# Moving the sums behind the norm, pinning adds, aligning pools, and a third seven-product unit per layer, in a two-layer encoder trunk

## The chip, the cores and the metric

The kernel runs on one core of a Trainium2 chip, as one program. The metric is device microseconds (us) of one execution. The engines of the core work side by side, each through its own list of instructions in order: TensorE (PE, matmuls; PEld is its weight loads), VectorE (DVE), ScalarE (ACT), GpSimd (POOL) and SyncE (SP, which here issues the loads). They wait for one another by semaphores.

## What is computed

An encoder trunk of two layers on 256 positions of 2048 channels, all in float32. Each layer has a mixer (pooling and attention in the first, a matrix memory, mLSTM, in the second) and a gated MLP, and this document is about the MLP:

```python
def conv_ffn(x, w_up, conv_w, conv_b, w_down):
    u = x @ w_up
    up = jnp.pad(u, ((0, 0), (1, 1), (0, 0)))
    c = conv_w.astype(u.dtype)
    u = c[0] * up[:, :-2] + c[1] * up[:, 1:-1] + c[2] * up[:, 2:] + conv_b.astype(u.dtype)
    gate, val = jnp.split(u, 2, axis=-1)
    return (jax.nn.silu(gate) * val) @ w_down
...
for layer in range(DEPTH):
    h = rms_norm(x, norm_mix[layer])
    ...
    x = x + mixed
    x = x + conv_ffn(rms_norm(x, norm_ffn[layer]), w_up[layer], conv_w[layer], conv_b[layer], w_down[layer])
```

`w_up` is 2048 x 11264 (two halves of 5632 = 44 tiles of 128), `w_down` 5632 x 2048.

## The kernel before

**Split numbers.** A float32 operand is kept as a high and a low part of a narrower format, and a product is three matmuls: high by high, high by low, low by high. Activations are split once per norm (`xx`, lines 282 and 285: high on ACT, low on DVE).

**The stream of weights.** All weights pass once through `Stream`, in the order in which PE uses them, as chunks of 128 x 1024 floats (512 KB). `load` (L89) issues the transfer on SP's queue into a raw tile `w`; `split` makes the high part on ACT (L105) and the low part on DVE (L106), in a tile `hl`. In an FFN layer there are seven raw tiles and five split ones; `ahead` keeps three split chunks ahead of PE's and issues a load five chunks ahead of the split.

**The FFN layer.** The 44 tiles of `w_up` are done in six groups of 4, 8, 8, 8, 8, 8 (`FCH`), each followed by its part of the down-projection, which is interleaved with the next group's up-projection. `_ffn_plan` writes the order out by hand as a list of slots, one weight chunk each: an up step ("n") has four slots of 16 matmuls, and yields one tile of gate and of value; a down step ("d") of a group and one of four column blocks has two or four slots of 12 matmuls. After an up step comes its tail: `gather` (L382, L383), the norm's row (L927), the convolution, the gate and the split of the result (L908 to L917). After a down step two residual adds (L392).

**Units of seven products.** For the last four tiles of two groups (`UNITS`: groups 2 and 4) the up-projection is not done by four up steps but as one 2 x 2 block product with seven block products in place of eight (`quads`). Its operands are sums of blocks of the activations, made once per layer by `sums()` (L935 to L951; tile `v`, split into `sx`), and sums of blocks of weights, made in place on the raw chunks by DVE in `split`: kind "sum" one add (L99), kind "chain" two (L102, which reads the sum of the chunk before, and L103). A unit has 28 chunks: eight pairs of sum and chain, then twelve of which eight are sums, 75% more loads than the sixteen that four up steps need. Each chunk serves two products of three matmuls (tile `p`). The partial results are put together on ACT and DVE (L993 to L1014), then turned by 16 transposes (L1026) and go through the same tails, by `finish`. `_ffn_plan` spreads a unit's chunks evenly among the slots between two places that `UNITS` gives, with a pause of three slots before the last twelve.

**The norm.** In an FFN layer PE starts before the norm's scale is known. `Norm.finish` computes it: a reduction (L298), a reciprocal square root (L224, a power on POOL at L226, L228 to L231) that gives `rcol`, two diagonals `dg` (L310), and one product with ones, `npr`, that gives the row `R` (L315). `n0` (L1085) is minus the first column of `rcol`.

**Who sets the order.** PE's instructions run as the program is written (`manual_schedule`). What is to happen beside the main stream (`norm.finish`, `sums_ready`, `finish`) is a generator in `Weave`: `add` gives it a delay, `tick` moves the time on with the matmuls issued (0.645 for four matmuls of an up step, 0.68 for three of a product) and runs one step of one generator that is due. The order of ACT's, DVE's and SP's instructions is made by the framework's scheduler from the program's data dependences and its own estimate of the time: it may put an instruction ahead of others that were written before it. `tc.keep_in_program_order(ins)` ties one instruction behind the one that was written just before it on the same engine.

Of the kernel before, what the change touches and what calls it, by code (L numbers as in the profile page):

```python
# [9 lines left out]
F32 = mybir.dt.float32  # L10
# [6 lines left out]
P = 128  # L17
# [47 lines left out]
class Stream:  # L65


    def __init__(self, nc, wpool, spool, srcs, load_ahead, split_ahead):
        self.nc, self.wpool, self.spool, self.srcs = nc, wpool, spool, srcs
        self.la, self.sa = load_ahead, split_ahead  # L70
        self.w, self.hl = {}, {}
        self.n_load = self.n_split = self.at = 0
        self.more = None
# [7 lines left out]
    def load(self, pieces=1):  # L81
        i = self.n_load
        src = self.srcs[i]
        kind, src = src if isinstance(src, tuple) else ("plain", src)
        width = src.shape[-1]
        n = width // pieces
        w = self.home(i, True).tile([P, CH * P], F32, tag="w", name=f"w{i}")
        for c in range(0, width, n):
            self.nc.sync.dma_start(w[:, c : c + n], src[:, c : c + n])  # L89
        self.w[i] = w, n, width, kind  # L90
        self.n_load += 1

    def split(self, then=None):
        i = self.n_split
        w, n, width, kind = self.w.pop(i)
        hl = self.home(i, False).tile([P, 2, CH * P], F32R, tag="hl", name=f"hl{i}")
        l, r = w[:, 0:512], w[:, 512:1024]
        if kind == "sum":
            self.nc.vector.tensor_add(r, r, l)  # L99
            self.sum = r  # L100
        if kind == "chain":
            self.nc.vector.tensor_add(l, l, self.sum)  # L102
            self.nc.vector.tensor_add(r, r, l)  # L103
        for c in range(0, width, n):
            (self.nc.vector.tensor_copy if i + c == 0 else self.nc.scalar.copy)(hl[:, 0, c : c + n], w[:, c : c + n])  # L105
            self.nc.vector.tensor_sub(hl[:, 1, c : c + n], w[:, c : c + n], hl[:, 0, c : c + n].bitcast(F32))  # L106
            then and then(c // n)
        self.hl[i] = hl
        self.n_split += 1

    def ahead(self, i, split=None):
        n = len(self.srcs)
# [14 lines left out]
class Weave:  # L127
# [6 lines left out]
    def add(self, gen, delay=0.0):  # L134
        self.q.append([self.t + delay, gen])
# [37 lines left out]
def trunk(ctx: ExitStack, tc: tile.TileContext, gx, xT, xn, call, catt, cml, weights, out):  # L173
    nc = tc.nc
    v, a, g, pe = nc.vector, nc.scalar, nc.gpsimd, nc.tensor
# [7 lines left out]
    wp = pool("wraw", 6)  # L183
    sp = pool("wsplit", 4)
    smp = pool("small", 2)
    sm1 = pool("small1", 1)
# [5 lines left out]
    gcol = cp.tile([P, NG], F32, tag="gcol", name="gcol")  # L192
    a_x = actp.tile([P, KT, S], F32, tag="B1", name="xT")
    x = xp.tile([P, 2, D], F32, tag="x", name="x")
    st = Stream(nc, wp, sp, weights, 5, 2)

    gx0 = actp.tile([P, NG + 2 * S], F32, tag="B0", name="gx0")
    ctx.enter_context(tc.manual_schedule(engines={mybir.EngineType.PE}))
# [11 lines left out]
    wv = Weave()  # L210
# [34 lines left out]
    class Norm:  # L245
# [48 lines left out]
        def finish(self):  # L294
            n = self.n
            yield from wv.wait(lambda: self.blocks == NB)
            s2 = smp.tile([P, 2], F32, tag="nsum", name=f"nsum{n}")
            v.tensor_reduce(s2, self.ss, AX.X, ALU.add)  # L298
            self.rcol = rsqrt(s2, 2, 1.0 / D, f"n{n}")
            yield 2.5  # L300
            if n % 2 == 0:
                rr = dram.tile([2, P], F32, tag="rr", name=f"rr{n}")
                g.dma_start(rr.rearrange("t p -> p t"), self.rcol)
                R = sm1.tile([P, S], F32, tag="R", name=f"R{n}")
                g.dma_start(R.rearrange("p (t q) -> p t q", t=2), rr.unsqueeze(0).to_broadcast([P, 2, P]))
                self.R = R
                return
            dg = sm1.tile([P, 2, P], F32, tag="dg", name=f"dg{n}")
            for t in range(2):
                v.tensor_scalar_mul(dg[:, t, :], ident, self.rcol[:, t : t + 1])  # L310
            yield 1.0
            pr = psp.tile([P, 512], F32, tag="ps", name=f"npr{n}")
            mm(pr[:, 0:S], ones, dg.rearrange("p a b -> p (a b)"), True, True)
            R = sm1.tile([P, S], F32, tag="R", name=f"R{n}")
            v.tensor_copy(R, pr[:, 0:S])  # L315
            self.R = R
# [571 lines left out]
    def ffn_layer(layer, norm, nxt):  # L888
        with ExitStack() as es:
# [4 lines left out]
            xsp = cp1 = lp(f"fs{layer}", 1)  # L894
# [35 lines left out]
            def sums():  # L930

                vv = actp.tile([P, 2, KT // 2, S], F32, tag="B1", name=f"v{layer}")
                for h in range(2):
                    ks = slice(8 * h, 8 * h + 8)
                    v.tensor_add(vv[:, 0], norm.xx[:, ks, 0, :].bitcast(F32), norm.xx[:, ks, 1, :].bitcast(F32))  # L935
                    yield 5.0
                    q = vv[:, 0].rearrange("p (a k) (t c) -> p a k t c", k=2, t=2)
                    a11, a21, a12, a22 = (q[:, :, k, t, :] for k in range(2) for t in range(2))
                    raw = vv[:, 1].rearrange("p k s -> p (k s)").rearrange("p (j a c) -> p j a c", j=4, a=4)
                    s1, s2, s3, s4 = (raw[:, j] for j in range(4))  # L940
                    v.tensor_sub(s1, a21, a22)
                    v.tensor_add(s3, a11, a21)
                    yield 3.0
                    v.scalar_tensor_tensor(s2, s1, -1.0, a11, ALU.mult, ALU.subtract)
                    v.tensor_sub(s4, s3, a12)
                    v.tensor_sub(s4, s4, a22)
                    yield 4.0
                    for j in range(4):
                        hi, lo = (sx[:, j, 4 * h : 4 * h + 4, i, :] for i in range(2))
                        a.copy(hi, raw[:, j])  # L950
                        v.tensor_sub(lo, raw[:, j], hi.bitcast(F32))  # L951
                        yield 2.0
# [15 lines left out]
            def quads(fs, gt, i0, name):  # L968
# [8 lines left out]
                r0, r1 = norm.rcol[:, 0:1], norm.rcol[:, 1:2]  # L977
                for p in range(m):
                    ends = p == 0, p == m - 1
                    hl = st.next()  # L980
                    if p == 0:
                        b1, b5 = bank(1), bank(5)
                    product(b1, block_of(2 * p, 0), hl, 0, *ends)
                    product(b5, sum_of(0, p), hl, 512, *ends)
                    yield
                    hl = st.next()
                    if p == 0:
                        b6, b4 = bank(6), bank(4)
                    product(b6, sum_of(1, p), hl, 0, *ends)
                    product(b4, block_of(2 * p + 1, 1), hl, 512, *ends)  # L990
                    if p == m - 1:
                        c12, c21, c22 = part(12), part(21), part(22)
                        a.activation(c12, b1, AF.Copy, scale=n0)  # L993
                        a.activation(c21, b1, AF.Copy, scale=r1)
                        a.activation(c22, b5, AF.Copy, scale=r1)
                        v.scalar_tensor_tensor(c12, b6, n0, c12, ALU.mult, ALU.add)
                    yield
# [21 lines left out]
            def finish(top, bottom, fs, gt, i0, name):  # L1019

                for n, f in enumerate(fs):
                    tr = psp.tile([P, 2, S], F32, tag="ps", name=f"tr{layer}_{f}")
                    for j in range(2):
                        for t, src in enumerate((top, bottom)):
                            c = (2 * j + n) * P
                            pe.transpose(tr[:, j, t * P : t * P + P], src[:, c : c + P], ident)  # L1026
                    u = tp.tile([P, 2, S], F32, tag="tb", name=f"tb_{layer}_{f}")
                    a.copy(u, tr)
                    tail(u, f, gt, i0 + n)
                    yield 2.5  # L1030

            def down_end(gt, b, kts):

# [44 lines left out]
            wv.add(norm.finish(), 4.0)  # L1078
            sx = xsp.tile([P, 4, KT // 2, 2, P], F32R, tag="sx", name=f"sx{layer}")

            n0 = xsp.tile([P, 1], F32, tag="n0", name=f"n0_{layer}")

            def sums_ready():
                yield from wv.wait(lambda: norm.R is not None)
                v.tensor_scalar_mul(n0, norm.rcol[:, 0:1], -1.0)  # L1085
                yield from sums()

            wv.add(sums_ready(), 8.0)
            st.la, st.sa, st.more = 7, 3, (lp(f"fw{layer}", 1), lp(f"fh{layer}", 1), st.at + len(_ffn_plan()))
            gts, run = {}, {}  # L1090
            for step in _ffn_plan():
                kind, c = step[:2]
                if kind != "d" and c not in gts:
# [78 lines left out]
    return np.concatenate(out)  # L1172


UNITS = {2: (1, 3), 4: (3, 5)}


def _ffn_plan():

    slots, begin = [], []  # L1180
# [9 lines left out]
    begin.append(len(slots))  # L1190
    here = [[] for _ in slots]
    m = KT // 2
    for c, (c0, c1) in UNITS.items():
        lo, hi = begin[c0] + 2, begin[c1] - 7
        one, two = 2 * m, m + m // 2
        step = (hi - lo - 3) / (one + two)
        for k in range(one + two):
            here[int(lo + k * step + (3 if k >= one else 0))].append(("s", c, 0))
# [148 lines left out]
```

## Time and profile before

| | us |
|---|---|
| three runs | 2223.16, 2224.29, 2226.46 (median 2224.29) |
| the profiled execution | 2224.29, its span (first to last instruction) 2222.0 |
| first FFN layer, first up matmul to first matmul of the mLSTM layer | 255.78 to 998.39 |
| second FFN layer, first up matmul | 1476.05 |
| matmuls of units, `p` | 672, from 322.9 to 2014 |
| granted TensorE clock, mean over the span | 0.995 |

The profile is one execution, taken by the hardware's profiler. Busy time is that of instructions at work; a row of a group gives line, engine, operation, what is written from what with shapes, how many, busy us, mean ns of one, and after the bar the idle time of the engine just before them with what ended it. Weights stream from memory at 198 GB/s on average over the span.

### The profile page before, as it was taken

How to read it: one execution, taken by the hardware profiler on the slowest of the kernel's cores; microseconds unless marked ns; L12 is line 12 of the kernel's file. 1: busy time of each engine (PE TensorE's matmuls, PEld its weight loads, DVE VectorE, ACT ScalarE, POOL GpSimd, SP SyncE). 2: the span in 40 equal slices, each digit the busy share in tenths (PEclk: the TensorE clock that was granted, in tenths of full speed). 3: DMA queues.
4: the chain of work that ended last, by engine and by line, in shares of the span. 5: the costliest groups of instructions: out<-in, count | busy, mean ns of one | idle time of the engine just before them, and what ended most of it. 6: DMA issues, size and time to landing. Idle time of an engine off the chain costs nothing.

```text
span 2222.0 us, 30399 instructions
## 1 busy us (share of the span) xinstructions
PE 2193.0 (99%) x11328; PEld 1864.8 (84%) x11328; DVE 1668.8 (75%) x2378; ACT 1228.3 (55%) x1744; POOL 28.1 (1%) x40
## 2 busy tenths in 40 slices
PE   9999899999999999999999999989999999999999
PEld 7888688888888888889888888868888888888887
DVE  7686778788787787666767666677878878778764
ACT  7675555556555565556555455545555655556552
POOL 0020000000000000000000000000000000000000
PEclk9999999999999999999999999999999999999999
DMA  8545546676666766556555555645667666676553
GB/s 317 187 157 181 170 164 215 209 239 215 217 221 222 222 198 191 188 157 206 163 193 184 185 180 167 198 162 165 213 210 238 217 215 220 223 223 199 190 190 123
DMA packets 124951, 440.88 MB, mean 198 GB/s; under 512 B 13851, under 2 KB 16195, under 8 KB 124803
## 3 DMA queue, kind: packets, MB, share of 16 engines
q1 hardware_dynamic: 121568, 434.93, 59.8%
q10 hardware_dynamic: 3074, 3.75, 0.7%
q8 instruction: 89, 1.46, 0.3%
q0 software_dynamic: 160, 0.26, 0.1%
q14 instruction: 60, 0.48, 0.1%
HBM read 436.74 MB, written 2.14 MB: 198 GB/s over the span
## 4 chain that ended last, share of the span: by engine, by line
PE 85%; DVE 6%; DMA 6%; issue 2%; ACT 0%; DVEq 0%; ACTq 0%
PE up L219 27%; PE dn L219 20%; PE op L219 8%; DMA w<-in_q 6%; PE p L219 5%; PE mv L219 4%; PE mq L219 4%; PE mk L219 4%; PE mo L219 4%; DVE hl L106 3%; PE qproj L219 3%; PE kproj L219 1%; PE pool L219 1%; PE vproj L219 1%; PE qk L219 1%
## 5 line engine op out<-in xcount | busy, mean ns | idle before, releaser
L106 DVE TENSOR_TENSOR hl<-w,hl 128x1024 fp32r<-128x1024 f32 (+1 forms) x820 | 992.3, 1217 | 295.8 <-ACT hl L105 291.7
L105 ACT CAST hl<-w 128x1024 fp32r<-128x1024 f32 (+1 forms) x819 | 851.7, 1047 | 570.6 <-PE up L219 185.5
L219 PE MATMUL up<-xx,hl 128*128 128x512 f32 (+1 forms) x4608 | 829.7, 338 | 1.9 <-DVE hl L106 1.9
L219 PEld LDWEIGHTS up<-xx,hl 128*128 128x128 f32 x4608 | 719.5, 189 | 114.6 <-DVE hl L106 4.8
L219 PE MATMUL dn<-hl,g 128*128 128x512 f32 x2064 | 485.0, 391 | 0.6 <-DVE hl L106 0.6
L219 PEld LDWEIGHTS dn<-hl,g 128*128 128x128 f32 x2064 | 385.2, 188 | 83.2 <-DVE hl L106 1.2
L908 ACT ACTIVATE y<-tb_up,cst 128x256 f32<-128x256 f32 x144 | 78.8, 595 | 84.6 <-DVE tb_up L927 83.5
L219 PE MATMUL p<-hl,sx 128*128 128x512 f32 x384 | 104.2, 393 | 0.0
L99 DVE TENSOR_TENSOR w<-w 128x512 f32<-128x512 f32 x64 | 44.3, 692 | 76.4 <-DMA w<-in_q 76.2
L382 ACT COPY tb_up<-up 128x512 f32<-128x512 f32 x72 | 42.2, 586 | 102.6 <-PE up L219 100.3
L219 PE MATMUL mk<-xx,hl 128*128 128x512 f32 (+1 forms) x512 | 92.2, 337 | 0.0
L219 PE MATMUL mq<-xx,hl 128*128 128x512 f32 (+1 forms) x512 | 92.1, 337 | 0.0
L219 PE MATMUL mv<-hl,xx 128*128 128x512 f32 (+2 forms) x480 | 91.7, 350 | 0.0
L219 PE MATMUL op<-hl,cat 128*128 128x512 f32 x384 | 91.6, 393 | 0.0
L219 PE MATMUL mo<-hl,xx 128*128 128x512 f32 x384 | 90.4, 391 | 0.0
L219 PE MATMUL op<-hl,mcat 128*128 128x512 f32 x384 | 89.5, 392 | 0.0
L219 PEld LDWEIGHTS mq<-xx,hl 128*128 128x128 f32 x512 | 79.2, 188 | 11.6
L219 PEld LDWEIGHTS mk<-xx,hl 128*128 128x128 f32 x512 | 79.0, 188 | 11.4
L219 PEld LDWEIGHTS mv<-hl,xx 128*128 128x128 f32 x480 | 78.3, 189 | 11.2
L219 PEld LDWEIGHTS op<-hl,mcat 128*128 128x128 f32 x384 | 71.5, 188 | 14.6
L219 PEld LDWEIGHTS mo<-hl,xx 128*128 128x128 f32 x384 | 71.0, 188 | 14.1
L219 PEld LDWEIGHTS op<-hl,cat 128*128 128x128 f32 x384 | 70.9, 188 | 14.1
(240 smaller groups left out, 1746.9 us busy)
## 6 DMA issues: line engine op xcount, KB each, us to landing
w<-in_up SPq DMA_DIRECT2D x288, 512.0 KB, 4.1
w<-in_dn SPq DMA_DIRECT2D x176, 512.0 KB, 4.3
w<-in_m_in SPq DMA_DIRECT2D x124, 512.0 KB, 4.1
w<-in_q SPq DMA_DIRECT2D x112, 512.0 KB, 4.2
w<-in_a_in SPq DMA_DIRECT2D x46, 512.0 KB, 4.3
w<-in_a_out SPq DMA_DIRECT2D x32, 512.0 KB, 3.4
w<-in_m_out SPq DMA_DIRECT2D x32, 512.0 KB, 3.5
w<-in_m_g SPq DMA_DIRECT2D x5, 432.0 KB, 3.5
```

The lines of the kernel that those rows point to most:

```text
L99: self.nc.vector.tensor_add(r, r, l)
L105: (self.nc.vector.tensor_copy if i + c == 0 else self.nc.scalar.copy)(hl[:, 0, c : c + n], w[:, c : c + n])
L106: self.nc.vector.tensor_sub(hl[:, 1, c : c + n], w[:, c : c + n], hl[:, 0, c : c + n].bitcast(F32))
L219: pe.matmul(out_, lhsT, rhs, start=start, stop=stop, skip_group_check=True)
L382: a.copy(tb, ps[:, :, 1, :])
L908: a.activation(y[:, j, :], u[:, j, :], AF.Identity, scale=cw(tl, 1), bias=cw(tl, 3))
```

## The change

Four edits. `sums_ready` is started with a delay of 14.0 in place of 8.0, and the first add of each half of `sums()` is tied behind the DVE instruction written before it. The adds on weight chunks move out of `split` into a method `sums`, which `split` calls for its own chunk if that is still to do, and, at its end, for the next chunk; each add is tied. `dg` is allocated 16 floats longer and `n0` 64 floats in place of 1. `UNITS` gets a third unit, of group 5, and places with slot offsets for all three; a unit's first chunk now waits (`late`, in the weave's time, not by a semaphore) until the tails of the unit before have been issued.

```diff
+    def sums(self, i):
+        if i in self.w and not self.w[i][4] and self.w[i][3] != "plain":
+            w, kind = self.w[i][0], self.w[i][3]
+            l, r = w[:, 0:512], w[:, 512:1024]
+            pin, add = self.tc.keep_in_program_order, self.nc.vector.tensor_add
+            if kind == "sum":
+                pin(add(r, r, l))
+                self.sum = r
+            if kind == "chain":
+                pin(add(l, l, self.sum))
+                pin(add(r, r, l))
+            self.w[i][4] = True

     def split(self, then=None):
         i = self.n_split
-        w, n, width, kind = self.w.pop(i)
+        self.sums(i)
+        w, n, width = self.w.pop(i)[:3]
...
-        if kind == "sum":
-            self.nc.vector.tensor_add(r, r, l)
-            self.sum = r
-        if kind == "chain":
-            self.nc.vector.tensor_add(l, l, self.sum)
-            self.nc.vector.tensor_add(r, r, l)
...
         self.hl[i] = hl
         self.n_split += 1
+        self.sums(i + 1)
...
-            dg = sm1.tile([P, 2, P], F32, tag="dg", name=f"dg{n}")
+            dg = sm1.tile([P, 2 * P + 16], F32, tag="dg", name=f"dg{n}")[:, : 2 * P]
+            dg = dg.rearrange("p (t q) -> p t q", t=2)
...
-                    v.tensor_add(vv[:, 0], norm.xx[:, ks, 0, :].bitcast(F32), norm.xx[:, ks, 1, :].bitcast(F32))
+                    tc.keep_in_program_order(
+                        v.tensor_add(vv[:, 0], norm.xx[:, ks, 0, :].bitcast(F32), norm.xx[:, ks, 1, :].bitcast(F32)))
...
                 for p in range(m):
                     ends = p == 0, p == m - 1
+                    if p == 0:
+                        wv.until(lambda: not late)
+                        late.update((0, 2))
...
                     tail(u, f, gt, i0 + n)
                     yield 2.5
+                late.discard((i0 - 4) % 4)
...
-            n0 = xsp.tile([P, 1], F32, tag="n0", name=f"n0_{layer}")
+            n0 = xsp.tile([P, 64], F32, tag="n0", name=f"n0_{layer}")[:, 0:1]
...
-            wv.add(sums_ready(), 8.0)
+            wv.add(sums_ready(), 14.0)
...
-            gts, run = {}, {}
+            gts, run, late = {}, {}, set()
...
-UNITS = {2: (1, 3), 4: (3, 5)}
+UNITS = {2: (1, 2, 2, 20), 4: (3, 0, 4, 20), 5: (4, 23, 5, 24)}
...
-    for c, (c0, c1) in UNITS.items():
-        lo, hi = begin[c0] + 2, begin[c1] - 7
+    for c, (c0, d0, c1, d1) in UNITS.items():
+        lo, hi = begin[c0] + d0, begin[c1] + d1
```

`begin[c]` is the slot at which group c starts: 0, 16, 56, 88, 136, 168 in both kernels, and the list ends at 216 before, at 200 after (four up steps of group 5 are gone), with sixteen slots of the last down step behind it.

More of the change, by code (lines that the diff above doesn't have):

```diff
@@ L65, with __init__ @@
 class Stream:
-    def __init__(self, nc, wpool, spool, srcs, load_ahead, split_ahead):
-        self.nc, self.wpool, self.spool, self.srcs = nc, wpool, spool, srcs
+    def __init__(self, tc, wpool, spool, srcs, load_ahead, split_ahead):
+        self.tc, self.nc, self.wpool, self.spool, self.srcs = tc, tc.nc, wpool, spool, srcs
         self.la, self.sa = load_ahead, split_ahead
@@ L89, in load @@
             self.nc.sync.dma_start(w[:, c : c + n], src[:, c : c + n])
-        self.w[i] = w, n, width, kind
+        self.w[i] = [w, n, width, kind, False]
         self.n_load += 1
+    def sums(self, i):
[10 more added lines that the diff above has]
+            self.w[i][4] = True
     def split(self, then=None):
         i = self.n_split
-        w, n, width, kind = self.w.pop(i)
+        self.sums(i)
+        w, n, width = self.w.pop(i)[:3]
         hl = self.home(i, False).tile([P, 2, CH * P], F32R, tag="hl", name=f"hl{i}")
-        l, r = w[:, 0:512], w[:, 512:1024]
-        if kind == "sum":
-            self.nc.vector.tensor_add(r, r, l)
-            self.sum = r
-        if kind == "chain":
-            self.nc.vector.tensor_add(l, l, self.sum)
-            self.nc.vector.tensor_add(r, r, l)
         for c in range(0, width, n):
@@ L194, in trunk @@
     x = xp.tile([P, 2, D], F32, tag="x", name="x")
-    st = Stream(nc, wp, sp, weights, 5, 2)
+    st = Stream(tc, wp, sp, weights, 5, 2)
     gx0 = actp.tile([P, NG + 2 * S], F32, tag="B0", name="gx0")
```

## The prediction

> **What bounds the kernel now.** I read the page's engine summary first, then the waits of TensorE (PE), then the order of instructions around the one long wait, then the chain of waits for the pace of each kind of matmul, and last the stretches in which VectorE (DVE) is fullest.
>
> ```profile
> span 2222.0 us, 30399 instructions
> PE 2193.0 (99%) x11328; PEld 1864.8 (84%) x11328; DVE 1668.8 (75%) x2378; ACT 1228.3 (55%) x1744; POOL 28.1 (1%) x40
> ```
>
> PE is busy all but 29 us, so the time is PE's work plus its few gaps. PE's waits (total us, times, longest):
>
> ```profile
> PE npr L219 <- DVE n L1085: 21.3, 2, 10.7
> PE up L219 <- DVE hl L106: 1.9, 5, 0.8
> ...
> PE dn L219 <- DVE hl L106: 0.6, 2, 0.4
> ```
>
> Almost all of it is one matmul, `npr`, which spreads the FFN norm's row over the partitions, once per FFN layer. The order of time around the first one (start, us, engine, line):
>
> ```profile
> 260.76 5.14 PE L219 MATMUL up<-xx,hl 128*128 128x512 f32 x28
> 276.56 1.19 PE L219 MATMUL npr<-dg,cst 128*128 128x256 f32 x2 [10.66 <-DVE n L1085]
> ```
>
> ```profile
> 257.18 2.28 DVE L935 TENSOR_TENSOR v<-xx 128x2048 f32<-128x2048 f32 x1
> ...
> 260.52 0.15 DVE L298 TENSOR_REDUCE nsum<-nss 128x2 f32<-128x8 f32 x1
> 260.59 0.68 DVE L941 TENSOR_TENSOR v<-v 128x512 f32<-128x512 f32 x1
> 261.19 0.69 DVE L942 TENSOR_TENSOR v<-v 128x512 f32<-128x512 f32 x1
> 261.79 1.22 DVE L106 TENSOR_TENSOR hl<-w,hl 128x1024 fp32r<-128x1024 f32 x1
> 262.93 0.48 DVE L285 SCALAR_TENSOR_TENSOR xx<-xt,gcol,xx 128x256 fp32r<-128x256 f32 x1
> 263.32 0.16 DVE L224 TENSOR_SCALAR rv_n<-nsum 128x2 f32<-128x2 f32 x1
> ...
> 267.72 0.15 DVE L228 TENSOR_TENSOR re_n<-ry_n 128x2 f32<-128x2 f32 x1
> ...
> 275.94 0.48 DVE L310 TENSOR_SCALAR dg<-cst,re_n 128x128 f32<-128x128 f32 x2
> ```
>
> The chain L298, L224, L228 to L231, L310 is seven tiny steps, but between every two of them DVE has been given a long one, mostly from `sums()` (L935 to L951). PE runs dry at about 265.9 and waits 10.66 us for a chain that is some 2 us of work. The clock then lags (columns: window, its us, busy us and counts of PE, PEld, DVE, ACT, POOL, granted clock, DMA share, GB/s):
>
> ```profile
> 275.00:280.00 5.00, 3.44 (x10) 2.90 (x11) 4.82 (x11) 1.64 (x3) 0.00 (x0) 0.50 0.00 0
> 280.00:285.00 5.00, 5.00 (x28) 4.35 (x28) 3.05 (x5) 3.16 (x5) 0.00 (x0) 0.93 0.01 3
> ...
> 1495.00:1500.00 5.00, 3.17 (x9) 2.63 (x10) 5.00 (x13) 1.91 (x4) 0.00 (x0) 0.50 0.00 0
> 1500.00:1505.00 5.00, 5.00 (x24) 4.36 (x23) 2.53 (x5) 2.56 (x4) 0.00 (x0) 0.73 0.00 0
> ```
>
> **The change, part by part.**
>
> *Sums behind the norm's row.* `sums_ready` starts 14 instead of 8 ticks into the layer, and the first add of each half (L935) is pinned behind whatever DVE instruction was traced before it. For the first half that is `n0`, which reads `rcol`, the end of the chain; the rest of `sums()` reads what L935 wrote. So nothing of `sums()` can stand between the chain's steps any more. What is left for DVE from 257.2 to 265.9, 8.7 us, are three or four splits (L106), four L285 and the chain. From row to row above, starts lie 0.60 apart for a 512-wide operation, 1.14 for a split and 0.39 for L285: 4 x 1.14 + 4 x 0.39 + about 1 = 7.1 us, which fits. The wait of 21.3 us goes, and so does the half clock: 3.44 us at 0.50 cost 1.7 and 5.00 us at 0.93 cost 0.35; 3.17 and 5.00 us at 0.50 and 0.73 cost 1.6 and 1.35. That is 5.0 in both layers. What may remain of the wait is 0 if the chain is through in time, 3 us a layer if each step still loses a split; I take 0.5.
>
> The Trainium skill (TensorE: Matmul & The Clock Gate, "HAM oscillation") says that gaps of PE over about 3.4 us let the gate fall back to half, and that it takes some 3.4 us of work to lift it again. By it the clock's part would be 2 x 1.7 = 3.4 us, 1.6 less than these rows give, and a leftover gap below 3.4 us would cost no clock; no row of this trace shows one between 1 and 10 us to try it on. I keep the rows.
>
> The sums themselves don't vanish: a half is 2.2 (L935) and nine operations of 0.6, 7.6 us, so 15.2 a layer, of which DVE did nearly all while PE stood. Now they lie beside the up-projections. The prices, from the groups (busy, mean ns, idle before), each less the 0.08 that starts overlap:
>
> ```profile
> L909 DVE SCALAR_TENSOR_TENSOR y<-tb_up,cst,y 128x255 f32<-128x255 f32 x144 | 63.6, 478 | 0.0
> ...
> L99 DVE TENSOR_TENSOR w<-w 128x512 f32<-128x512 f32 x64 | 44.3, 692 | 76.4 <-DMA w<-in_q 76.2
> ...
> L915 DVE TENSOR_TENSOR y<-y 128x256 f32<-128x256 f32 x88 | 36.9, 420 | 1.1 <-ACT y L914 0.9
> ```
>
> A slot (one weight chunk) of an up step costs DVE a split, 1.14, and a quarter of the tail (two at 0.61, four at 0.40, two at 0.34), 0.87: 2.01 us. A down slot costs 1.14 + 2 x 0.6 / 4 = 1.44. A unit's chunk costs 2.05 in its first sixteen (a split and 1.5 adds of 0.61) and 1.55 in the last twelve. The second half of the sums is needed by the unit's ninth chunk, slot 33. From slot 4 to there DVE has 28 up slots, 2 down slots, 8 unit chunks and the sums: 56.3 + 2.9 + 16.4 + 15.2 = 90.8 us, while PE has 28 x 2.79 + 2 x 2.74 + 8 x 1.38 = 94.6 (paces below). 96% full: between 0 and some 4 us a layer; I take 1.5, since three split chunks (8 us) are kept ready ahead of PE. What queues behind a pinned L935 is splits and tails; PE waits for the splits first.
>
> *The third unit.* PE's paces, from the chain of waits and the order of time:
>
> ```profile
> 885.12 22.29 PE up L219 x128
> 907.41 10.99 PE dn L219 x48
> ```
>
> ```profile
> 329.90 0.86 PE L219 MATMUL p<-hl,sx 128*128 128x512 f32 x3
> 330.60 0.86 PE L219 MATMUL p<-hl,xx 128*128 128x512 f32 x3
> 331.30 5.72 PE L219 MATMUL up<-xx,hl 128*128 128x512 f32 x32
> ...
> 533.16 0.60 PE L1026 MATMUL tr<-cst,c 128*128 128x128 f32 x4
> 533.52 2.36 PE L219 MATMUL up<-xx,hl 128*128 128x512 f32 x12
> ```
>
> An up step is 64 matmuls, 11.15 us (2.79 a slot); a down slot is 10.99 / 4 = 2.74. A unit chunk is six matmuls: 1.40 us from start to start here, 12 x 10.99 / 48 / 2 = 1.37 at the down pace; 1.38. Four up steps (44.6) become 28 chunks (38.6) and 16 transposes (four take 0.36: 1.4). A unit saves 4.6 +- 0.5, two units 9.
>
> It costs 12 more chunks per layer, loaded and split. By the plan's arithmetic the layer's chunks 4 and 5 begin at slots 136 and 168, so the new unit lies on slots 159 to 192, one unit chunk to 1.07 slots, where the old two have one to 2.14 and 2.43 (now 1.96 and 2.32). That stretch has 16 up slots, 17 down slots and 28 unit chunks. PE: 44.6 + 46.6 + 38.6 = 129.8 us. DVE: 32.2 + 24.5 + 32.8 + 18.6, five operations on the partial results (3.1) and the four tails of the unit before (4 x 2.28 = 9.1): 120.3 us, 93%. Can DVE do that without holding PE? Windows of the present units, same columns:
>
> ```profile
> 438.00:548.00 110.00, 109.38 (x554) 92.19 (x554) 91.67 (x125) 67.03 (x89) 0.00 (x0) 1.00 0.70 228
> ...
> 460.00:480.00 20.00, 20.00 (x97) 16.65 (x96) 17.28 (x23) 11.36 (x14) 0.00 (x0) 1.00 0.83 275
> 480.00:500.00 20.00, 20.00 (x103) 16.95 (x102) 14.62 (x17) 10.14 (x12) 0.00 (x0) 1.00 0.69 224
> 500.00:520.00 20.00, 20.00 (x104) 16.99 (x103) 13.87 (x16) 9.93 (x12) 0.00 (x0) 1.00 0.77 254
> 520.00:540.00 20.00, 20.00 (x105) 17.04 (x104) 18.97 (x29) 14.70 (x23) 0.00 (x0) 1.00 0.68 219
> 540.00:560.00 20.00, 20.00 (x101) 16.86 (x101) 20.00 (x36) 13.78 (x23) 0.00 (x0) 1.00 0.52 176
> ```
>
> For 40 us it ran at 97% with PE at 20.00 of 20, but over 110 us nothing has asked more than 83% of it. I take 2 us of waits a layer, from 0 at the one end to 15 at the other (120.3 / 0.83 = 145). The loads: 61 chunks of 524,288 bytes in 130 us are 246 GB/s, and 460 to 520 moved 251 without holding PE, so transfers are costed at nothing; without that cover each late chunk would show as DVE waiting.
>
> *Adds of weights pinned a chunk ahead.* Today the scheduler lets them run ahead of DVE's queue to where a load has not landed:
>
> ```profile
> DVE w L99 <- DMA w<-in_q: 76.2, 57, 3.7
> DVE w L102 <- DMA w<-in_q: 35.9, 23, 3.5
> ```
>
> ```profile
> w<-in_q SPq DMA_DIRECT2D x112, 512.0 KB, 4.2
> ```
>
> That is 112 us of DVE, 28 in each unit, 1.4 a wait, behind which splits and tails queue. Pinned behind the split of the chunk before, the add comes later in the queue; loads are issued five chunks ahead of splits, so at 2.1 us a chunk some 10 us pass against 4.2 for landing. The gain is DVE's idle time, not PE's: at most the 2.5 us of PE waits on L106; I take 1. In return a "sum" chunk's buffer is held until the "chain" add, one of seven buffers for some two chunks more: nothing, while 10 stays above 4.2.
>
> *Aligned pools, and `late`.* `dg` and `n0` only move what lies behind them. No row here tells a shifted tile from another, so I cost it at nothing and bound it by the longest single wait on a split, 0.8 us, either way. `late` holds a unit's start until the tails of the last are issued; the unit before ends at slot 153, its tails 10 ticks (4 slots) on, before 159: nothing, and a few us if they slip.
>
> **The sum.** 2222.0 - 21.3 - 5.0 - 9 = 2186.7. New waits 2 x (0.5 + 1.5 + 2) = 8, less 1: 2193.7. The profiled execution took 2224.29 us, 2.3 more than its span, and is itself the median of the three runs. So 2196.
>
> **The rivals.**
>
> *VectorE becomes the bound in the third unit.* For: 93% wanted where a long stretch has had 83%. Against: part of that 83% was its waits on loads, which the pins remove, and 97% was held for 40 us. In the middle, at 88%, 120.3 / 0.88 = 136.7, 7 us a layer: 10 more than the forecast, 2206; at 83% 2222.
>
> *The norm's row stays late*, so the change doesn't do what its first words say: the chain's steps are each placed behind a split or a tail still. For: the scheduler puts something between any two dependent steps. Against: without the sums there is little to put there. Half the wait and clock left gives 13 more, 2209; all of it 2221.
>
> *Slower: the pinned adds stall DVE in order.* A pinned add waits for its load and everything behind it waits too. If each of the 24 summed chunks of the dense unit waits the present 1.4 us, DVE needs 120.3 + 34 = 154 where PE has 130: 24 us a layer, and with the sums squeezed likewise by the first unit (16 adds' chunks, 22 us, against 4 us of room: 18 a layer) 84 less the 7 counted comes to 2273; the dense unit alone to 2240. It decides (the time passes 2224) from a mean wait of about 0.8 us if both stretches have it, 1.1 if only the dense one does. Against: the loads' lead of 10 us.
>
> **How the numbers follow.** Forecast 0.63 (2186 to 2204); VectorE as bound 0.18 (2204 to 2221); the row stays late 0.08; slower 0.11. The range from 2185 to 2214 holds the first, two thirds of the second and most of the third. The least, with no new wait and the old 2.5 gone, is 2186.5. A change under 0.2% (4.4 us) can't be told from none: faster 0.87, same 0.02, slower 0.11.
>
> **What would show it.** Right: `npr` gone from PE's waits or under 1 us, no granted clock of 0.50 around 280 and 1500; 1008 `p` matmuls (six units of 168, now four) and 64 up steps (now 72) at the paces above; DVE's waits on loads at L99 and L102 far under 112 us although there are half again as many; DVE near 18.5 of 20 over the 130 us that end some 66 us (8 slots and 16 of the last down step) before the layer does. Wrong: PE waits on L106 of more than 15 us in all, or L935 ahead of L310 again. If `p` chunks take over 1.45 us, the unit saves nothing; if DVE still waits over 1 us an add, the slower rival is at work.

## The result, and the profile after

| | median us | runs | ratio to before, 95% interval |
|---|---|---|---|
| before, same session | 2225.38 | 2223.16 to 2227.27 (4) | |
| changed | 2195.32 | 2194.49 to 2195.72 (4) | 0.9867 [0.9854, 0.9881] |

30 us faster, 0.7 from the forecast of 2196. The page of the changed kernel (span, engine busy time):

```profile
span 2192.2 us, 30245 instructions
...
PE 2176.0 (99%) x11184; PEld 1851.8 (84%) x11184; DVE 1731.4 (79%) x2460; ACT 1254.0 (57%) x1776; POOL 29.2 (1%) x40
```

First the norm's row: PE and DVE in order of time at the first FFN layer (lines have moved: L298 is L306 now, L310 L319, L935 L945, the split L113).

```profile
261.24 5.15 PE L227 MATMUL up<-xx,hl 128*128 128x512 f32 x28
266.22 0.60 PE L227 MATMUL npr<-dg,cst 128*128 128x256 f32 x2
266.47 33.79 PE L227 MATMUL up<-xx,hl 128*128 128x512 f32 x192
```

```profile
258.93 0.16 DVE L306 TENSOR_REDUCE nsum<-nss 128x2 f32<-128x8 f32 x1
259.12 0.17 DVE L232 TENSOR_SCALAR rv_n<-nsum 128x2 f32<-128x2 f32 x1
260.11 0.16 DVE L236 TENSOR_TENSOR re_n<-ry_n 128x2 f32<-128x2 f32 x1 [0.82 <-POOL ry_n L234]
...
262.96 0.47 DVE L319 TENSOR_SCALAR dg<-cst,re_n 128x128 f32<-128x128 f32 x2
263.35 0.15 DVE L1099 TENSOR_SCALAR n<-re_n 128x1 f32<-128x1 f32 x1
263.41 2.28 DVE L945 TENSOR_TENSOR v<-xx 128x2048 f32<-128x2048 f32 x1
```

The chain from L306 to L319 takes 4.5 us in place of 15.9, `dg` is ready 2.8 us before PE wants it, and the first sum stands behind `n0`, as tied. PE goes through `npr` without a gap. But PE has new waits, all at unit products `p`, and they were not there before (total us, times, longest):

```profile
PE p L227 <- DVE hl L113: 7.6, 7, 3.0
PE p L227 <- ACT hl L112: 3.5, 2, 3.3
```

Most of them, 9.3 of the 11.1 us, lie in the new, dense unit of the two layers. In the first layer (windows: us, busy us of PE, PEld, DVE, ACT, POOL, clock, DMA share, GB/s):

```profile
800.00:820.00 20.00, 19.27 (x88) 15.55 (x86) 18.34 (x25) 10.09 (x14) 0.00 (x0) 1.00 0.68 227
820.00:840.00 20.00, 15.64 (x68) 12.87 (x69) 14.17 (x15) 9.25 (x10) 0.00 (x0) 0.83 0.64 216
```

DVE is not full in the second window, 14.17 of 20, and no longer waits for a load: the rows of L99 and L102 waiting for `in_q` are gone from the list. In their place ACT waits for the adds:

```profile
ACT hl L112 <- DVE w L99: 98.1, 56, 4.2
...
ACT hl L112 <- DVE w L103: 38.8, 29, 3.1
```

### The profile page after: what moved, and what is told of

It is laid out like the page before. It is cut to its first block, busy times and chain, and to the rows that moved or that the text cites. A ratio compares the mean times of both kernels' runs of the same rounds, so it can differ in the third digit from the quotient of the medians.

```text
span 2192.2 us, 30245 instructions
## 1 busy us (share of the span) xinstructions
PE 2176.0 (99%) x11184; PEld 1851.8 (84%) x11184; DVE 1731.4 (79%) x2460; ACT 1254.0 (57%) x1776; POOL 29.2 (1%) x40
## 4 chain that ended last, share of the span: by engine, by line
PE 92%; DVE 6%; issue 1%; ACT 1%; ACTq 0%; DVEq 0%
PE up L227 28%; PE dn L227 20%; PE p L227 9%; PE op L227 8%; PE mv L227 4%; PE mq L227 4%; PE mk L227 4%; PE mo L227 4%; PE qproj L227 3%; DVE hl L113 3%; PE kproj L227 1%; PE pool L227 1%; PE vproj L227 1%; PE av L227 1%; PE qk L227 1%
## 5 line engine op out<-in xcount | busy, mean ns | idle before, releaser
L113 DVE TENSOR_TENSOR hl<-w,hl 128x1024 fp32r<-128x1024 f32 (+1 forms) x844 | 1017.7, 1218 | 319.5 <-ACT hl L112 312.4
L112 ACT CAST hl<-w 128x1024 fp32r<-128x1024 f32 (+1 forms) x843 | 873.6, 1048 | 646.1 <-PE up L227 118.9
L227 PE MATMUL up<-xx,hl 128*128 128x512 f32 (+1 forms) x4096 | 737.7, 337 | 0.0
L227 PEld LDWEIGHTS up<-xx,hl 128*128 128x128 f32 x4096 | 643.0, 189 | 99.9
L227 PE MATMUL p<-hl,sx 128*128 128x512 f32 x576 | 157.0, 393 | 9.5 <-DVE hl L113 6.0
L227 PEld LDWEIGHTS p<-hl,sx 128*128 128x128 f32 x576 | 104.1, 188 | 30.4 <-DVE hl L113 8.1
L227 PE MATMUL p<-hl,xx 128*128 128x512 f32 x432 | 119.3, 393 | 1.5 <-DVE hl L113 1.5
L227 PEld LDWEIGHTS p<-hl,xx 128*128 128x128 f32 x432 | 78.1, 189 | 16.4 <-DVE hl L113 2.5
L227 PEld LDWEIGHTS mq<-xx,hl 128*128 128x128 f32 x512 | 79.3, 188 | 11.6
L391 ACT COPY tb_up<-up 128x512 f32<-128x512 f32 x64 | 37.5, 586 | 81.1 <-PE up L227 78.7
L917 ACT ACTIVATE y<-tb_up,cst 128x256 f32<-128x256 f32 x128 | 70.0, 595 | 24.2 <-DVE tb_up L936 22.4
```

The source lines that it names most:

```text
L227: pe.matmul(out_, lhsT, rhs, start=start, stop=stop, skip_group_check=True)
L391: a.copy(tb, ps[:, :, 1, :])
L917: a.activation(y[:, j, :], u[:, j, :], AF.Identity, scale=cw(tl, 1), bias=cw(tl, 3))
```

## The experiments

Differences below are of medians. The spread of before (2220 to 2229 over all sessions) makes up most of each ratio's interval. The runs of one changed kernel agree within 0.2 to 3.2 us (e8: 5.7), and the median of before moves by 2.1 from session to session, so a difference of 2 us between sessions is not told from none.

| run | sums tied | units | adds on weights | aligned | median us | ratio, 95% interval |
|---|---|---|---|---|---|---|
| e8 | delay only | 2 | free | no | 2225.76 | 1.0004 [0.9994, 1.0013] |
| e9 | tie only | 2 | free | no | 2193.24 | 0.9856 [0.9841, 0.9870] |
| e1 | yes | 2 | free | no | 2193.39 | 0.9856 [0.9841, 0.9871] |
| e2 | no | 3 | free | no | 2215.32 | 0.9954 [0.9938, 0.9971] |
| e10 | yes | 2 | free | yes | 2186.90 | 0.9829 [0.9814, 0.9843] |
| e5 | yes | 2 | tied | yes | 2188.61 | 0.9834 [0.9821, 0.9848] |
| e3 | yes | 3 | free | yes | **2180.11** | 0.9796 [0.9782, 0.9809] |
| changed | yes | 3 | tied | yes | 2195.32 | 0.9867 [0.9854, 0.9881] |
| e4 | yes | 3 | tied | no | 2202.52 | 0.9898 [0.9884, 0.9911] |
| e12 | yes | 3 | tied | `n0` only | 2202.41 | 0.9906 [0.9890, 0.9923] |
| e6 | yes | 3, spread | tied | yes | 2190.56 | 0.9842 [0.9829, 0.9856] |
| e7 | yes | 3 | tied two ahead | yes | 2182.37 | 0.9808 [0.9794, 0.9823] |
| e11 | yes | 4 | free | yes | 2198.81 | 0.9882 [0.9865, 0.9898] |

### The sums behind the row: e1, e8, e9

On the kernel before: e1 has both lines, e8 the second alone, e9 the first alone.

```diff
-                    v.tensor_add(vv[:, 0], norm.xx[:, ks, 0, :].bitcast(F32), norm.xx[:, ks, 1, :].bitcast(F32))
+                    tc.keep_in_program_order(
+                        v.tensor_add(vv[:, 0], norm.xx[:, ks, 0, :].bitcast(F32), norm.xx[:, ks, 1, :].bitcast(F32)))
...
-            wv.add(sums_ready(), 8.0)
+            wv.add(sums_ready(), 14.0)
```

> The kernel before with the first edit alone: the sums of activations started at 14 ticks, their first add tied. Theory: this is the largest part, 26 us (21.3 of the wait of npr, 5.0 of the half clock), less about 1 us a layer of new waits under the up-projections: 2197 to 2203, npr under 1 us among PE's waits, no window at a clock of 0.5. Rival: the 15 us of sums only change place and hold the splits up elsewhere: PE waits on splits (L106) of 8 us or more and a time over 2206.

> The kernel before with the delay of 14 ticks alone, nothing tied. Theory: the scheduler moves the adds forward whatever the delay is, as their inputs are there, so npr still waits 15 us or more in all: 2216 to 2226. Rival: the delay alone puts them behind the row: npr under 2 us, 2198 to 2204.

> The kernel before with the first add of each half tied, the delay left at 8. Theory: the tie is the whole of it (what is written before it reads the end of the norm's chain): npr under 2 us, 2196 to 2203, within 2 us of the run with both. Rival: the later start is needed for the sums not to hold up the first splits: 3 us or more above the run with both.

The tie is the whole of it: 2193.24 with it alone, 2193.39 with both. With the delay alone the sums are written later, yet in the compiled program every engine's instructions stand in the order of the kernel before, and `npr` waits as it did (PE's waits in e8):

```profile
PE npr L219 <- DVE n L1085: 21.3, 2, 10.7
```

The gain, 31 us, is more than the 26 of the theory. In e1's list of PE's waits only the warm-up matmul is left:

```profile
PE wps L243 <- DVE pad L611: 1.2, 1, 1.2
```

So no wait on a split remains, old or new. The old ones come to 2.5 us by the matmuls, whose modelled ends cover part of a gap, and to 6.0 by the weight loads. In the kernel before:

```profile
PEld up L219 <- DVE hl L106: 4.8, 7, 1.2
PEld dn L219 <- DVE hl L106: 1.2, 2, 0.7
```

The spans differ by 31.0 (2222.0 and 2191.0); less 21.3 and 5.0 of clock, 4.7 are left for them, between the two readings and nearer to that of the weight loads. The 15 us of sums per layer are hidden entirely. That the sums tied in time also freed those splits was not tested apart.

### The third unit alone: e2

The kernel before with the new `UNITS`, its slot offsets and `late`, nothing else of the change.

> The kernel before with the third unit alone (its places, and the wait for the earlier unit's tails); adds on weights free, sums of activations as before. Theory: without the tied adds DVE idles for loads in the dense unit, some 28 us a unit on top of 120 us of work in 130, so PE waits on splits by 15 us a layer or more there: 2235 or more, slower than before. Rival: the ties matter little, the waits are those of the changed kernel (11 us and a clock dip of 2): 2225 - 9 + 13 = 2229 or less, down to 2217.

The theory fell and even the rival was too pessimistic: 2215.32, 9.3 less than before in its session (2224.65), which is what was reckoned for PE's work alone. Behind `npr`, PE's only waits on splits are

```profile
PE dn L219 <- DVE hl L106: 2.7, 4, 1.0
```

DVE does idle for loads at the free adds (137 us over six units), and it hardly matters.

### The adds free again: e3

```diff
-            pin, add = self.tc.keep_in_program_order, self.nc.vector.tensor_add
+            pin, add = (lambda i: i), self.nc.vector.tensor_add
...
         self.n_split += 1
-        self.sums(i + 1)
```

> The changed kernel with the adds on weight chunks free again, written in the split of their own chunk. Theory: DVE waits on loads at the adds come back (over 100 us in all) and the dense units hold PE: PE waits on splits over 25 us, 2207 or more. Rival: the ties only move the waiting from DVE to ACT: 2192 to 2199.

The edit takes away both the tie and the writing of each add one chunk early. The result is opposite in sign to the theory, and beyond the rival: 15.2 us **faster** than the changed kernel, and the fastest run of all. Its PE and DVE waits:

```profile
PE dn L226 <- DVE hl L113: 1.8, 2, 1.3
...
PE p L226 <- DVE hl L113: 0.4, 1, 0.4
```

```profile
DVE w L99 <- DMA w<-in_q: 91.3, 63, 4.9
DVE w L102 <- DMA w<-in_q: 26.7, 19, 2.8
```

118 us of DVE waiting for loads are back, and PE waits 2.2 us, 8.9 less than in the changed kernel (by the weight loads 3.6 against 14.5, 10.9 less). The changed kernel's trace also records half clock for 6.8 us behind the long wait, 1.5 of them in the next gap, which is about 2.7 us lost; e3's trace has none. That is 11.6 to 13.6 of the 15.2. The dense unit of the first layer, changed kernel first, then this one:

```profile
782.00:912.00 130.00, 124.91 (x597) 104.25 (x596) 111.15 (x144) 72.68 (x90) 0.31 (x1) 0.97 0.71 235
```

```profile
782.00:912.00 130.00, 129.56 (x636) 109.17 (x635) 116.39 (x152) 79.35 (x99) 0.31 (x1) 1.00 0.77 247
```

DVE is fuller, 116.39 of 130 (90%), and PE hardly notices. So the old waits of DVE were slack, and the ties took something else away.

### Are ties costly everywhere, or only where units are dense? e5, e10, e6

e5 is the changed kernel, e10 is e3, each with two units in their old places: `UNITS = {2: (1, 2, 3, -7), 4: (3, 2, 5, -7)}`. e6 is the changed kernel with `{2: (1, 2, 2, 20), 4: (2, 22, 4, 2), 5: (4, 7, 5, 24)}`.

> The changed kernel with the two units of before in their old places. Theory: a unit saves 4.5 us of PE, but the dense one gives 9.3 us of waits and 1.7 of clock back over both layers, so the third unit nets about nothing: 2192 to 2198. Rival: it is worth its 9 us and the waits would have come anyway: 2202 to 2206.

> Two units, adds free, aligned, sums tied: the fourth corner to two units tied (2188.6), three tied (2195.3), three free (2180.1). Theory: the ties cost something only where units lie dense, so this is 2186.5 to 2189, and the third unit is worth 7 to 9 us with free adds. Rival: the ties cost each unit alike (5 us a unit and layer pair): 2177 to 2181, and the third unit is worth nothing even with free adds.

> The changed kernel with the same three units spread more evenly: the second on slots 78 to 138, the third on 143 to 192, one chunk to 2.04 and 1.64 slots in place of 2.32 and 1.07. Theory (density does it): the waits of the dense stretch, 9.3 us and 1.7 of clock, mostly go: 2184 to 2189. Rival (the tied adds block ACT's queue wherever a unit runs, whatever its density): waits of 8 us or more stay and 2193 or more.

Two units: 2188.61 tied, 2186.90 free, 1.7 for the ties, which is not told from nothing between two sessions (PE waits 1.1 us on splits in e5 and none in e10). Three: 2195.32 and 2180.11, 15.2. The ties cost where units lie dense. With free adds the third unit is worth 6.8 us; with tied ones it loses 6.7, more than the "nets about nothing" of the theory, so e5 lies below both its ranges. e6 came out between the two expectations. Density does make the waits on splits, which fall from 11.1 us to 1.8, but the new places made another wait (PE, then DVE's splits):

```profile
PE p L227 <- ACT tb L1041: 6.2, 2, 3.1
PE p L227 <- DVE hl L113: 1.8, 3, 1.2
```

Both long waits lie where the second unit starts, at slot 78, four slots behind the first one's last chunk (the changed kernel leaves fourteen): its products take the four PSUM banks (where matmuls write; `psp`, L189 before) that the first still needs for its turned tiles, until ACT has copied them (L1041).

### What the tie does: e7

The order of time in the changed kernel, where PE waits longest. PE, DVE, ACT:

```profile
816.68 2.94 PE L227 MATMUL up<-xx,hl 128*128 128x512 f32 x16
822.90 0.78 PE L227 MATMUL p<-hl,sx 128*128 128x512 f32 x1 [3.28 <-ACT hl L112]
825.14 1.22 PE L227 MATMUL p<-hl,sx 128*128 128x512 f32 x2 [1.46 <-DVE hl L113]
```

```profile
816.13 0.69 DVE L102 TENSOR_TENSOR w<-w,w 128x512 f32<-128x512 f32 x1
816.73 1.28 DVE L401 TENSOR_TENSOR x<-x,dn 128x512 f32<-128x512 f32 x2
817.92 1.22 DVE L113 TENSOR_TENSOR hl<-w,hl 128x1024 fp32r<-128x1024 f32 x1
819.06 0.69 DVE L99 TENSOR_TENSOR w<-w 128x512 f32<-128x512 f32 x1
819.66 0.69 DVE L103 TENSOR_TENSOR w<-w 128x512 f32<-128x512 f32 x1
820.99 2.36 DVE L113 TENSOR_TENSOR hl<-w,hl 128x1024 fp32r<-128x1024 f32 x2 [0.64 <-ACT hl L112]
823.26 0.69 DVE L102 TENSOR_TENSOR w<-w,w 128x512 f32<-128x512 f32 x1
823.86 1.22 DVE L113 TENSOR_TENSOR hl<-w,hl 128x1024 fp32r<-128x1024 f32 x1
```

```profile
812.76 2.95 ACT L112 CAST hl<-w 128x1024 fp32r<-128x1024 f32 x3 [1.82 <-issue]
819.91 2.94 ACT L112 CAST hl<-w 128x1024 fp32r<-128x1024 f32 x3 [4.20 <-DVE w L99]
```

L99 comes only after the split of the chunk before (817.92, as the tie wants). The high part that needs it is next in ACT's queue: ACT idles 4.20 us, then makes three in a row, and DVE, having idled 0.64, does the low parts. PE starts again at 822.90, when the third high part is done, and goes on at 825.14, after the low part of 823.86.

So PE does not wait for the chunk whose add was late, but for the third in the row. The compiled program numbers the chunks in PE's order: the split at 817.92 is that of chunk 315, the adds behind it are those of 316 (L99) and 314 (L103), and ACT's three high parts are 316, 317, 314. The chunk that PE wants, 314, stands behind three later ones in DVE's queue, and behind the same three in ACT's. It is so at the second layer's longest wait too (764 behind 765 to 767), and at three others the chunk stands behind two later ones; these five chunks have 10.5 of PE's 11.1 us. In e3 only one chunk of the FFN layers stands behind two later ones, and none behind three.

The theory saw a loop: split, add, high part, split, add, through two engines, with a chunk's lead and no more. e7 gives it two:

```diff
         self.sums(i + 1)
+        self.sums(i + 2)
```

> The changed kernel with the tied adds made two chunks ahead of their split in place of one. The runs so far: with the adds free the changed kernel takes 2180.1, so the ties cost 15. Theory: tied a single chunk ahead they close a loop, split of the chunk before, add, high part on ACT, split, add, of about 1.14 + 0.6 to 1.2 + 1.05 + 1.14 = 3.9 to 4.5 us for a pair of chunks where PE takes 2.76 + 1.38 = 4.14; one chunk more of lead opens it: ACT's waits on L99 and L103 (137 us) fall to less than a third, PE's waits (11 us) under 3, 2180 to 2184. Rival: DVE is simply too full in the dense stretch for any fixed order: PE waits of 8 us or more and 2191 to 2197.

2182.37, 13 us less than the changed kernel. PE's waits are down from 11.1 to 2.1, ACT's from 137 to 50 (the expectation said less than a third; it is a little over):

```profile
PE p L228 <- DVE hl L113: 2.1, 5, 0.6
```

```profile
ACT hl L112 <- DVE w L103: 36.4, 22, 3.6
ACT hl L112 <- DVE w L99: 13.5, 8, 2.5
```

Neither DVE's fill (115.75 us of 782 to 912, where e3 has 116.39) nor a tie as such is at fault, then; with two chunks of lead the cost is gone. In e7 no chunk stands behind more than two later ones. Whether it is the loop's pace that costs or the place of the chunk in the two queues was not taken apart.

### The addresses: e4, e12

e4 takes both paddings out of the changed kernel, e12 that of `dg` alone. All engines have the same instructions in the same order in the three; only addresses differ.

```diff
-            dg = sm1.tile([P, 2 * P + 16], F32, tag="dg", name=f"dg{n}")[:, : 2 * P]
+            dg = sm1.tile([P, 2 * P], F32, tag="dg", name=f"dg{n}")
...
-            n0 = xsp.tile([P, 64], F32, tag="n0", name=f"n0_{layer}")[:, 0:1]
+            n0 = xsp.tile([P, 1], F32, tag="n0", name=f"n0_{layer}")
```

> The changed kernel with dg and n0 at their old sizes. Theory: nothing, within 2 us of the changed kernel (2193 to 2197.5). Rival: shifted tiles cost splits or transfers something: 3 us or more slower, and a mean split or median landing longer than 1218 ns and 4.1 us.

> The changed kernel with n0 padded and dg at its old size; every engine has the same instructions in the same order as in the changed kernel and in the run with neither (2202.5), only addresses differ. With neither, the fifth split tile, from which PE reads weights in an FFN layer, starts 32 bytes past a multiple of 64 and its down matmuls run at 233.5 ns from start to start against 226.7; with both, every tile of an FFN layer starts at a multiple of 256. With n0 alone they start at odd multiples of 64. Theory (a multiple of 64 bytes is enough): 2195 to 2198, the down matmuls of all five tiles at 227. Rival (128 or 256 is needed): 2200 to 2204, the fifth tile slow still.

e4 is 7.2 us slower, e12 7.1: the rival both times, though not by splits or transfers. PE itself runs slower. Two down slots in e4, then two in the changed kernel:

```profile
656.48 5.71 PE L227 MATMUL dn<-hl,g 128*128 128x512 f32 x24
```

```profile
654.61 5.60 PE L227 MATMUL dn<-hl,g 128*128 128x512 f32 x24
```

and all of them (the groups' busy us and mean ns), in the same order:

```profile
L227 PE MATMUL dn<-hl,g 128*128 128x512 f32 x2064 | 491.2, 392 | 0.0
```

```profile
L227 PE MATMUL dn<-hl,g 128*128 128x512 f32 x2064 | 487.5, 390 | 0.0
```

Sorted by which of the five split tiles the weights came from, the down matmuls of the first FFN layer lie apart, from start to start, by these paces (for each chunk the mean of its eleven steps, then the median over a tile's chunks, worked out from the trace's matmuls in order; start of the fifth tile modulo 256 from the compiled program, the other four start at a multiple of 256 in all three):

| | fifth tile starts at | tiles 1 to 4, ns | tile 5, ns |
|---|---|---|---|
| e4, neither padded | 224 | 226.6 to 228.9 | 233.4 |
| e12, `n0` padded | 192 | 226.6 to 228.5 | 233.4 |
| changed | 0 | 226.6 to 226.7 | 226.7 |

A down matmul costs 6.7 ns more when the tile from which PE streams its 512 columns starts 192 or 224 past a multiple of 256; a multiple of 64 is not enough, and whether 128 would be wasn't tried. (The slowest of tiles 1 to 4, at 228.9 and 228.5, is the one used next after the fifth; why is open.)

That is not all of the 7 us. A fifth of the 2064 down matmuls, 413, stream from the fifth tile: 2.8 us. By the groups' busy time, e4 less the changed kernel, the down matmuls make 3.7 us, the up matmuls 1.3 and the products 2.7 (`p` with `sx` 1.7, shown below, e4 first; with `xx` 1.0):

```profile
L227 PE MATMUL p<-hl,sx 128*128 128x512 f32 x576 | 158.7, 396 | 9.2 <-DVE hl L113 5.8 <-ACT hl L112 3.2
L227 PE MATMUL p<-hl,sx 128*128 128x512 f32 x576 | 157.0, 393 | 9.5 <-DVE hl L113 6.0 <-ACT hl L112 3.5
```

The products of the first layer are slower from all five tiles, 230.6 to 233.4 ns in e4 against 226.8 to 228.6, and their other operand, `sx`, has moved as well: it starts at 192 in e4 and e12, at 0 in the changed kernel. Which operand slows them was not taken apart.

### Four units: e11

e3 with `UNITS = {2: (1, 2, 2, 4), 3: (2, 8, 3, 17), 4: (3, 21, 4, 24), 5: (4, 27, 5, 26)}`.

> Four units per layer (groups 2 to 5, slots 18 to 60, 64 to 105, 109 to 144, 147 to 178), adds free, aligned, sums tied. Theory: PE is the bound and each unit gives 4.6 us a layer, less waits; DVE would have to be some 91% full over the layer (634 + 16 of 713 us): 2171 to 2178. Rival: DVE is the bound at that fill: PE waits on splits of 15 us or more and 2182 or more.

2198.81: slower than three units by 18.7. The fourth unit takes 9 us off PE's work by the reckoning above, but PE's list of waits comes to 20 us against 2 (by the weight loads 27 against 4), and the trace records half clock for 13.7 us, about 10 of them at work, so 5 us lost. -9 + 20 - 2 + 5 = 14 by the matmuls, -9 + 27 - 4 + 5 = 19 by the weight loads. Half of the waits are at unit products that wait for ACT's copies, as in e6, not for splits:

```profile
PE p L226 <- ACT tb L1040: 9.8, 2, 5.6
PE dn L226 <- ACT g L924: 4.2, 2, 2.1
PE p L226 <- DVE hl L113: 1.9, 2, 1.5
```

## Why the prediction was right, and where it was not

The time is right to 0.7 us, but by luck: two of its four parts are wrong, and the errors cancel. From the runs above, each step between neighbours:

| part | predicted | measured |
|---|---|---|
| sums behind the row | -21.3 - 5.0, +4 of new waits | -31.3 (e1) |
| third unit, adds free | -9, +4 of waits | -9.3 (e2), -6.8 (e10 to e3) |
| ties on the weights' adds | -1 | +1.7 with two units, **+15.2** with three |
| aligned pools | 0, at most 0.8 | **-6.5** (e1 to e10), -7.2 (e4 to changed) |

-31.3 - 6.5 - 6.8 + 15.2 = -29.4, where 30.1 were measured. Against the forecast the parts are off by -9.0, -1.8, +16.2 and -6.5, together by -1.1. e1 and e10, like e4 and the changed kernel, have the same instructions in the same order on every engine.

*Sums behind the row.* Right in mechanism: the wait and the half clock are gone, the chain ends before PE needs it. Mis-sized: the new waits, 0.5 and 1.5 us a layer, are 0, and the old waits on splits, of which the prediction counted 1 us as the gain of the ties on weights, went with the sums: 4.7 us. The delay, which the prediction named beside the tie, does nothing.

*Third unit.* The work of PE was right (9.3), and so was the choice of stretch: dense, and DVE at 90% in e3 where 93% was reckoned. That DVE "has had 83%" was no limit.

*Ties.* This step failed: "The gain is DVE's idle time, not PE's: at most the 2.5 us". It looked at what the tie does to DVE's waits for loads, and that part came true (112 us to none). It did not ask who waits for the add: the high part on ACT, and behind it, in ACT's own queue, the high parts of other chunks, that of the chunk which PE wants next among them. In place of a gain of 1 us the ties cost 15.2. The rival that named the pinned adds had the right place and the wrong engine, DVE stalling on a load; no such stall occurred.

*Aligned pools.* This step failed too: "cost it at nothing and bound it by the longest single wait". An address does not make a wait; it changes the pace of each of some hundreds of matmuls, and a list of waits cannot show that. The kernel before has it too (sorted by split tile as above, its fifth tile's down matmuls take 233.4 ns), and the prediction, which took one mean pace for each kind of matmul, did not sort them.

*The clock.* Both dips went with the wait, as forecast. The other runs add what the kernel before could not show, shorter gaps, and no single border comes out of them. After 3.28 us and, closely behind, 1.46 us the changed kernel's window 820 to 840 is at 0.83, while the second layer's longest gap, 2.99 us, left the clock at 1.00:

```profile
2000.00:2020.00 20.00, 16.81 (x80) 13.74 (x79) 18.77 (x28) 11.30 (x16) 0.00 (x0) 1.00 0.63 224
```

In e11 a gap of 2.09 us before 941.93 (2.48 from start to start of the matmuls) was followed by half clock, and one of the same length before 2154.56 was not:

```profile
940.00:945.00 5.00, 3.07 (x8) 2.35 (x9) 2.20 (x4) 0.89 (x3) 0.00 (x0) 0.72 0.79 235
...
2150.00:2155.00 5.00, 2.91 (x13) 1.99 (x12) 4.83 (x9) 2.08 (x5) 0.00 (x0) 1.00 0.73 217
2155.00:2160.00 5.00, 5.00 (x24) 4.12 (x23) 2.22 (x3) 2.05 (x2) 0.00 (x0) 1.00 0.37 119
```

The Trainium skill (TensorE: Matmul & The Clock Gate, "HAM oscillation") puts the border at about 3.4 us. The gap of 2.09 us at 941.93 does not fit it. So the prediction's sentence that a leftover gap below 3.4 us would cost no clock does not hold here; no term of its sum rests on it.

The version to keep is e3: all of the change but the ties on the weights' adds, 2180.11 us.

## What to carry to other kernels

Idle time of an engine with slack is not a cost, and an order that removes it can be one: before tying an instruction behind another, ask which queue stands behind its reader, and if one chunk of lead makes that queue wait, try two. A chain of tiny steps that PE waits for needs its competitors tied behind its end; writing them later in the program did nothing here, under a scheduler that reorders. Where two parts of a change are expected to be small, take them apart all the same: here +15.2 and -6.5 lay hidden in a total that came out as forecast.

## What the runs showed of the hardware

The pace of a float32r matmul can depend on where the tile that it streams starts: the down matmuls of 512 columns run at 226.7 ns at a multiple of 256 bytes and at 233.4 at 192 or 224 past one, while the splits (1218 ns on average) and the weights' loads (4.1 to 4.3 us in the FFN layers) are the same. With the products, where `sx` moved as well, and the up matmuls the shift is 7 us of 2195, and no list of waits shows it.

Ahead of the program's last few us, the traces record half clock in stretches of 3.41 us (e6, twice; e11, twice), 6.83 (changed, e11), 10.24 and 13.65 (before): 1, 2, 3 and 4 times 3.41. They followed gaps of PE from 2.09 to 10.66 us, and gaps of 2.09 and 2.99 us passed without one.
